# Hybrid attention and mLSTM encoder layer: more projection work ahead of the short sequence's gates and state products, and the long sequence's small loads moved from SyncE's queue to GpSimd's

## The chip, the cores and the metric

One core of a Trainium2 chip runs the whole layer. The metric is the device time of one execution in microseconds (us); lower is better.

## The reference, cut to what matters

Two sequences, 1024 ("short", s = 0) and 2048 tokens ("long", s = 1), each with 16 learned meta tokens ahead, go through the same layer in float32. One input projection feeds two branches, a neighbourhood attention (8 heads of 64) and a bidirectional mLSTM (4 heads of 128); both results are gated, projected, merged and projected once more.

```python
proj = xn @ w_in + b_in                      # 1024 -> 6672 columns
na_q, na_k, na_v, na_z, ml_qk, ml_v, ml_z, ml_o, ml_g, mg = split(proj)
ya = (neighbourhood_attention(na_q, na_k, na_v, rpb) * silu(na_z)) @ w_a
yb = (mlstm(ml_qk, ml_v, ml_g, ml_o, conv_w, head_g) * silu(ml_z)) @ w_b
ga, gb = split(sigmoid(mg))
y = (ga * ya + gb * yb) @ w_out
return h + rmsnorm(y, g_post)
# mlstm, chunk by chunk, both directions: the state is a decayed sum of weighted products
#   C_new = fs * C + isc * (w * v)^T k      with w, fs, isc from the gates ml_g
#   h = (S v + e * C q) / max(|den|, exp(-m))
```

## The kernel before, in words

TensorE's order is written by hand (`manual_schedule` for PE); the other engines' orders come from a scheduler that simulates the program. PE's order is woven in `run()` out of two generators. `dense` yields the big projections piece by piece: groups of input projections, the Strassen-like gate products (lines 787 to 790 and 988 to 990), and last the "final" blocks. Each final block takes 512 tokens: output gates times the two branches' projections (128x512 matmuls at lines 218 to 220, from `yh`, `yl`), then the product with `w_out` (128x256 matmuls at lines 1953 to 1955). A dense matmul triple computes one float32-like product out of high and low halves (`xh`, `xl`, `whl`). `sparse` yields the four mixer stages in the order of `STEPS`: mLSTM of the short sequence, attention of the short, mLSTM of the long, attention of the long. At every `yield` of `sparse`, dense pieces worth that cost (times `A_S`, 1.15 for the short and 0.91 for the long sequence) are put into PE's order before the sparse work goes on; they cover the time in which VectorE, ScalarE and the DMAs prepare the next sparse step. Costs are counted with 0.235 us for a 128x512 matmul and 0.12 for a 128x256.

An mLSTM stage has three parts, which this case names by their functions.

- `ml_gates`: the gate inputs are loaded as `g_t` (lines 1320, 1321), cumulative sums are taken by matmuls with a triangle (line 1347), and per-chunk values are transposed on PE (line 1400 for `g_uR`, line 1409 for e and w).
- `ml_states`, per head and per 256 tokens: a convolution input `raw` (line 1437) and values `va` (line 1507) are loaded, the keys are convolved (`kf`, line 1534), transposed on PE (line 1574), split into `kth` (ScalarE, line 1577) and `ktl` (VectorE, line 1578), and multiplied with the weighted values `vwh`, `vwl` (six matmuls `sm<-vwh,kth`, lines 218 to 220). `ktl` is the input of the third, sixth of these.
- `ml_outputs`, per head and per 256 tokens: loads of `raw`, `kf` (line 1620), two `um` (line 1626), and per 512 tokens `tog`, `szg` (lines 1638, 1639); `kh` (ScalarE, line 1665), scores `sc<-q,kh` (line 1703), the decay matrix on VectorE and ScalarE out of `um` (lines 1673 to 1723), products with `v2`.

In the attention, the last step of each head pair and 512 tokens is PE's line 1288, then `yg` by ScalarE (line 1295) and VectorE (1302, 1304), and a store to `ya` (line 1305). `yload` loads it again for the final block (`yl`, line 1850; `yh` by ScalarE, line 1871; the low half by VectorE, line 1855). Final block 3 of the long sequence is the last and needs `ya` of the last 512 tokens. In `final`, the products with `yb` (k = 4 to 7) stand ahead of those with `ya` (k = 0 to 3). If a needed `yl` hasn't been ordered yet, `final` yields True, and `run` goes on with sparse work alone until it has.

Nearly all loads and stores are issued by SyncE (SP) in program order, among them the dense side's weights (`whl`, lines 304 and 310) and activations (`xh`, `xl`, lines 944 and 953); GpSimd (POOL) issues some 200 others.

Of the kernel before, what the change touches and what calls it, by code (L numbers as in the profile page):

```python
# [18 lines left out]
P = 128  # L19
# [9 lines left out]
BIG = 1e30  # L29
# [9 lines left out]
BL = CB * P  # L39
# [96 lines left out]
A_N, A_D, A_A, A_G, A_S = (1.08, 0.93), 1.63, 1.79, 1.3, (1.15, 0.91)  # L136


class K:
# [1169 lines left out]
    def ml_gates(self, s, keep, mp, res):  # L1309
        nc = self.nc  # L1310
# [4 lines left out]
        kt = lambda n: keep.tile([P, NC_, 4], F32, name=n, bufs=1)  # L1315
        gt = t("g_t", [P, NC_, 16])
        for d in range(2):
            nc.gpsimd.memset(gt[:, 0, 8 * d:8 * d + 4], -BIG)
            nc.gpsimd.memset(gt[:, 0, 8 * d + 4:8 * d + 8], 1.0e4)
        nc.sync.dma_start(gt[:NM, 0, :], self.GA[s][0:NM, :])  # L1320
        nc.sync.dma_start(gt[:, 1:, :], self.GA[s][NM:, :].rearrange("(c p) g -> p c g", p=P))
        yield 11.0
        gv = gt.rearrange("p c (d k h) -> p d k c h", d=2, k=2)
        lf = t("g_lf", [P, 2, NC_, 4])
        e = t("g_e", [P, 2, NC_, 4])
# [18 lines left out]
        def one(d):  # L1344
            l2 = lf[:, d].rearrange("p c h -> p (c h)")
            pb = self.psum("sm", [P, 512])
            nc.tensor.matmul(pb[:, :NR], self.tri[:, d, :], l2, start=True, stop=True)
            bT = t(f"g_b{d}", [P, NC_, 4])
            nc.vector.tensor_copy(bT.rearrange("p c h -> p (c h)"), pb[:, :NR])
            aT = kt(f"g_a{d}")  # L1350
            nc.vector.tensor_tensor(aT, gv[:, d, 0], bT, op=ALU.subtract)
            aTf = aT.rearrange("p c h -> p (c h)")
            yield
            pa = self.psum("sm", [P, 512])
            nc.tensor.transpose(pa[:NR, :P], aTf, self.ident)
            aR = t("g_aR", [NR, P], bufs=2)
            nc.scalar.activation(aR, pa[:NR, :P], AF.Copy)
            yield
            cm = t("g_cm", [NR, P], bufs=2)
            rv = (lambda x: x) if d == 0 else (lambda x: x[:, ::-1])  # L1360
            nc.vector.tensor_tensor_scan(out=rv(cm), data0=rv(aR), data1=rv(aR), initial=-3.0e38, op0=ALU.max, op1=ALU.max)
            end = P - 1 if d == 0 else 0
            pg = self.psum("sm", [P, 512])
            nc.tensor.matmul(pg[0:1, :NR], self.ones[:, 0:1], l2, start=True, stop=True)
            rg = t("g_rg", [1, NR], bufs=2)
            nc.scalar.activation(rg, pg[0:1, :NR], AF.Copy)
            yield
            px = self.psum("sm", [P, 512])
            nc.tensor.transpose(px[0:1, :NR], cm[:, end:end + 1], self.ident[:NR, :NR])
            ra = t("g_ra", [1, NR], bufs=2)  # L1370
            nc.vector.tensor_tensor(ra, px[0:1, :NR], rg, op=ALU.add)
            me = t("g_me", [1, NR], bufs=2)
            mpv = t("g_mp", [1, NR], bufs=2)
            nc.gpsimd.memset(mpv, 0.0)
            yield
            for h in range(4):
                w = slice(h, NR, 4)
                nc.vector.tensor_tensor_scan(out=rv(me[:, w]), data0=rv(rg[:, w]), data1=rv(ra[:, w]), initial=0.0,
                                             op0=ALU.add, op1=ALU.max)
            if d == 0:  # L1380
                nc.vector.tensor_copy(mpv[:, 4:], me[:, :NR - 4])
            else:
                nc.vector.tensor_copy(mpv[:, :NR - 4], me[:, 4:])
            yield
            pm = self.psum("sm", [P, 512])
            nc.tensor.transpose(pm[:NR, 0:1], mpv, self.ident[0:1, 0:1])
            mpc = t("g_mpc", [NR, 1], bufs=2)
            nc.vector.tensor_copy(mpc, pm[:NR, 0:1])
            uR = t("g_uR", [NR, P], bufs=2)
            nc.vector.tensor_scalar(uR, cm, mpc, -1.0, op0=ALU.max, op1=ALU.mult)  # L1390
            nc.sync.dma_start(self.UD[s][d][:, :], uR)
            uend = t("g_ue", [NR, 1], bufs=2)
            nc.vector.tensor_copy(uend, uR[:, end:end + 1])
            nc.scalar.activation(cm, uR, AF.Exp, bias=mpc)
            nc.scalar.activation(aR, aR, AF.Exp, bias=uend)
            fs = t("g_fs", [NR, 1], bufs=2)
            nc.scalar.activation(fs, uend, AF.Exp, bias=mpc)
            yield
            pu = self.psum("sm", [P, 512])
            nc.tensor.transpose(pu[:, :NR], uR, self.ident[:NR, :NR])  # L1400
            em = kt(f"g_em{d}")
            nc.vector.tensor_tensor(em.rearrange("p c h -> p (c h)"), pu[:, :NR], bT.rearrange("p c h -> p (c h)"), op=ALU.subtract)
            nc.scalar.activation(em, em, AF.Exp)
            dg = t("g_dg", [NR, NR], bufs=2)
            nc.vector.tensor_scalar(dg, self.ident[:NR, :NR], fs, None, op0=ALU.mult)
            yield
            for name, x in (("e", cm), ("w", aR)):
                pe = self.psum("sm", [P, 512])
                nc.tensor.transpose(pe[:, :NR], x, self.ident[:NR, :NR])
                eT = kt(f"g_{name}T{d}")  # L1410
                nc.vector.tensor_copy(eT.rearrange("p c h -> p (c h)"), pe[:, :NR])
                out[d][name] = eT
                yield
            pf = self.psum("sm", [P, 512])
            nc.tensor.matmul(pf[:, :NR], self.ones[:NR, :], dg, start=True, stop=True)
            fsb = kt(f"g_fb{d}")
            nc.vector.tensor_copy(fsb.rearrange("p c h -> p (c h)"), pf[:, :NR])
            out[d].update(a=aT, em=em, f=fsb)
# [8 lines left out]
    def conv_load(self, src, c0, n, T):  # L1427

        nc = self.nc
        L = NM + T  # L1430
        raw = self.keep.tile([P, BL + 2], F32, name="raw", bufs=2)
        a, b = max(c0 - 1, 0), min(c0 + n + 1, L)
        if a > c0 - 1:
            nc.gpsimd.memset(raw[:, 0:1], 0.0)
        if b < c0 + n + 1:
            nc.gpsimd.memset(raw[:, n + 1:n + 2], 0.0)
        nc.sync.dma_start(raw[:, a - c0 + 1:b - c0 + 1], src[:, a:b])
        return raw

    def conv(self, raw, h, is_k, n):  # L1440
# [13 lines left out]
    def ml(self, s):  # L1454
        tc, nc = self.tc, self.nc
        T, self.seq = SEQLEN[s], s
        NB = T // BL
        with tc.tile_pool(name=f"mg{s}", bufs=1, side="right", reuse_waits="tile") as keep:
            with tc.tile_pool(name=f"mt{s}", bufs=1, side="right", reuse_waits="tile") as mp:
# [43 lines left out]
    def vload(self, s, h, tok, np_, nch):  # L1503
        nc = self.nc
        va = self.vas[0]
        self.vas = self.vas[1:] + [va]
        nc.sync.dma_start(va[:np_, :nch, 0:P],
                          self.MV[s][tok:tok + np_ * nch, h * P:(h + 1) * P].rearrange("(c p) f -> p c f", p=np_))
        return va

    def ml_states(self, s, h, g, NB, sts):

        nc, mp = self.nc, self.mlp
# [53 lines left out]
        for i in range(N):  # L1567
            n, c0 = seq[i]
            nch, np_ = max(1, n // P), min(n, P)
            conv_a(i + 1)  # L1570
            kf = kfs.pop(i)
# [9 lines left out]
            conv_b(i + 1)  # L1581
            vsplit(i + 1)
            yield A_D
            vwh, vwl = vws.pop(i)
            if not c0:
                pd = self.psum("sm", [P, 512])
# [4 lines left out]
            b = (c0 - NM) // BL  # L1591
# [5 lines left out]
            for j in range(CB - 1, -1, -1):  # L1597
# [6 lines left out]
                if cc > 0:  # L1604
                    nc.vector.scalar_tensor_tensor(sts[(cc - 1) // CB][:, (cc - 1) % CB, 130:260], sts[b][:, j, 130:260],
                                                   g[1]["f"][:, 1 + cc, h:h + 1], pd[:, 130:260], op0=ALU.mult, op1=ALU.add)
            yield A_D

    def ml_outputs(self, mp, s, h, g, NB, sts, norms):

# [4 lines left out]
        def load(b):  # L1615
            if b < NB:
                t0 = b * BL
                raws[b] = self.conv_load(self.MQ[s][h], NM + t0, BL, SEQLEN[s])
                kfs[b] = kf = self.keep.tile([P, BL], F32, name="kf", bufs=2)
                nc.sync.dma_start(kf, self.KF[s][h][:, t0:t0 + BL])  # L1620
                ums[b] = []
                for d in range(2):
                    um = mp.tile([P, CB, P], F32, name="um", bufs=4)
                    ud = self.UD[s][d]
                    src = bass.AP(tensor=ud.tensor, offset=ud.offset + ((1 + b * CB) * 4 + h) * P, ap=[[0, P], [4 * P, CB], [1, P]])
                    nc.sync.dma_start(um, src)
                    ums[b].append(um)

        def vnext(b):
# [3 lines left out]
        def gates(b):  # L1633

            if b % 2:
                tzs[b // 2] = [mp.tile([P, 4, P], F32, name=n, tag="tz", bufs=2) for n in ("tog", "szg")]
                x, z = tzs[b // 2]
                nc.sync.dma_start(x, self.TO[s][(b - 1) * BL:(b + 1) * BL, h * P:(h + 1) * P].rearrange("(c p) f -> p c f", p=P))
                nc.sync.dma_start(z.rearrange("p a b -> p (a b)"), self.SZ[s][h][:, (b - 1) * BL:(b + 1) * BL])

        def conv_a(b):
            if b < NB:
# [564 lines left out]
```

## Time and profile before

| what | value |
|---|---|
| time, median of 3 runs | 2666.21 us (2662.89 to 2666.56) |
| the profiled execution's own time | 2665.67 us |
| its span | 2663.9 us, 46683 instructions |
| granted TensorE clock, mean | 0.997 |
| PE busy | 2635.1 us (99%) |
| VectorE (DVE), ScalarE (ACT), GpSimd (POOL) busy | 72%, 53%, 7% of the span |
| DMA | 800.47 MB, 300 GB/s; SP's queue q1 697.24 MB, POOL's queue q0 100.25 MB |

PE is busy nearly all the time, so the time is PE's work plus the gaps in it. A row of the list of waits says: the engine and line that waited, what it waited for, the microseconds in total, how often, and the longest. In the timeline a row is start, duration, engine, line, operation, tile out<-in, and in brackets the idle time before it and what ended it. In the table of stretches a row gives each engine's busy time and, as PEclk, the clock granted to TensorE as a share of full speed, then the share of the DMA engines and GB/s.

### The profile page before, as it was taken

The page shows a single profiled execution, that of the slowest core. Times are in us where ns is not written, and L with a number is a line of the kernel's source. Part 1 is how long each engine was busy: PE and PEld are TensorE (multiplying, and loading weights), DVE is VectorE, ACT ScalarE, POOL GpSimd, SP SyncE. Part 2 cuts the span into 40 slices and gives each one's busy share as a digit, 9 for nine tenths or more (in the row PEclk, how much of TensorE's full clock was granted, in tenths as well). Part 3 has the DMA queues.
Part 4 walks back from the last instruction along what each step waited for, and adds up shares of the span by engine and source line. Part 5 has one row for each costly group of instructions (what it writes and reads, how often), then busy time and mean ns, then how long its engine had stood idle before and what let it go on. Part 6 is the DMA issues. An engine that isn't in the chain of part 4 may idle for free.

```text
span 2663.9 us, 46683 instructions
## 1 busy us (share of the span) xinstructions
PE 2635.1 (99%) x15928; PEld 2328.5 (87%) x15928; DVE 1915.0 (72%) x5070; ACT 1423.7 (53%) x3292; POOL 196.3 (7%) x418
## 2 busy tenths in 40 slices
PE   9999999999999999999999999999999999999998
PEld 7898897899988999878888888878889898989888
DVE  5655678788776877546676776857478889797854
ACT  5423555555445554546665676656366655656521
POOL 0111131011301124000000000000000000000000
PEclk9999999999999999999999999999999999999999
DMA  9899988799866999978889998899899899898965
GB/s 371 328 332 337 332 302 303 279 339 344 313 218 242 352 324 309 317 230 268 261 269 342 370 295 260 282 348 324 275 323 321 283 306 286 284 306 266 326 244 206
DMA packets 393517, 800.47 MB, mean 300 GB/s; under 512 B 50528, under 2 KB 173360, under 8 KB 389440
## 3 DMA queue, kind: packets, MB, share of 16 engines
q1 hardware_dynamic: 361728, 697.24, 77.9%
q0 software_dynamic: 31552, 100.25, 10.2%
q8 instruction: 126, 2.06, 0.3%
q14 instruction: 111, 0.91, 0.1%
HBM read 543.72 MB, written 253.60 MB: 299 GB/s over the span
## 4 chain that ended last, share of the span: by engine, by line
PE 91%; DMA 4%; DVE 3%; ACT 1%; issue 1%; SPq 0%; DVEq 0%; ACTq 0%
PE pj L218 10%; PE pj L220 10%; PE pj L219 10%; PE pj L988 8%; PE pj L990 8%; PE pj L989 8%; PE pj L787 5%; PE pj L789 5%; PE pj L788 5%; PE pj L1954 3%; PE pj L1953 3%; PE pj L1955 3%; PE sm L1288 3%; PE tr L1273 2%; PE sm L220 1%; PE sm L219 1%
## 5 line engine op out<-in xcount | busy, mean ns | idle before, releaser
L218 PE MATMUL pj<-xh,whl 128*128 128x512 f32 (+1 forms) x960 | 369.7, 385 | 3.1 <-ACT xh L445 2.5
L220 PE MATMUL pj<-xh,whl 128*128 128x512 f32 (+1 forms) x960 | 361.0, 376 | 0.0
L219 PE MATMUL pj<-xl,whl 128*128 128x512 f32 (+1 forms) x960 | 360.3, 375 | 0.2 <-DVE xl L446 0.2
L787 PE MATMUL pj<-whl,xh 128*128 128x256 f32 (+1 forms) x1152 | 329.0, 286 | 0.0
L789 PE MATMUL pj<-whl,xl 128*128 128x256 f32 (+1 forms) x1152 | 325.3, 282 | 0.0
L788 PE MATMUL pj<-whl,xh 128*128 128x256 f32 (+1 forms) x1152 | 324.9, 282 | 0.0
L1953 PE MATMUL pj<-whl,mh 128*128 128x256 f32 x768 | 218.3, 284 | 1.1 <-DMA whl<-w 1.1
L787 PEld LDWEIGHTS pj<-whl,xh 128*128 128x128 f32 x1152 | 217.1, 188 | 0.4
L788 PEld LDWEIGHTS pj<-whl,xh 128*128 128x128 f32 x1152 | 217.0, 188 | 0.2
L789 PEld LDWEIGHTS pj<-whl,xl 128*128 128x128 f32 x1152 | 217.0, 188 | 0.0
L1954 PE MATMUL pj<-whl,mh 128*128 128x256 f32 x768 | 216.3, 282 | 0.0
L1955 PE MATMUL pj<-whl,mlo 128*128 128x256 f32 x768 | 215.5, 281 | 0.0
L218 PEld LDWEIGHTS pj<-xh,whl 128*128 128x128 f32 x960 | 181.2, 189 | 35.3 <-ACT xh L445 3.4
L220 PEld LDWEIGHTS pj<-xh,whl 128*128 128x128 f32 x960 | 181.2, 189 | 35.0
L219 PEld LDWEIGHTS pj<-xl,whl 128*128 128x128 f32 x960 | 181.8, 189 | 30.4 <-issue 1.0
L988 PE MATMUL pj<-xh,whl 128*128 128x512 f32 x512 | 206.7, 404 | 1.3 <-ACT pj L1005 1.1
L990 PE MATMUL pj<-xh,whl 128*128 128x512 f32 x512 | 202.0, 395 | 0.0
L989 PE MATMUL pj<-xl,whl 128*128 128x512 f32 x512 | 201.1, 393 | 0.0
L1280 DVE TENSOR_TENSOR pts<-tr,pts 96x384 fp32r<-96x384 f32 (+2 forms) x192 | 118.6, 618 | 63.8 <-ACT pts L1275 62.4
L1275 ACT ACTIVATE pts<-tr 96x384 fp32r<-96x384 f32 (+2 forms) x192 | 103.5, 539 | 101.7 <-PE tr L1273 101.1
L218 PE MATMUL pj<-yh,whl 128*128 128x512 f32 x384 | 154.1, 401 | 0.0
L219 PE MATMUL pj<-yl,whl 128*128 128x512 f32 x384 | 151.5, 395 | 0.7 <-DVE yl L1855 0.7
(380 smaller groups left out, 6824.9 us busy)
## 6 DMA issues: line engine op xcount, KB each, us to landing
whl<-w SPq DMA_DIRECT2D x131, 1024.0 KB
whl<-q SPq DMA_DIRECT2D x112, 512.0 KB
w<-whl SPq DMA_DIRECT2D x36, 1024.0 KB
wraw<-wu SPq DMA_DIRECT2D x48, 512.0 KB
gt<-st SPq DMA_DIRECT2D x96, 256.0 KB
tg<-gt SPq DMA_DIRECT2D x96, 256.0 KB
q<-po POOLq DMA_DIRECT2D x26, 512.0 KB, 7.3
xt<-xt SPq DMA_DIRECT2D x24, 512.0 KB
```

The lines of the kernel that those rows point to most:

```text
L218: mm(out, ah, bh, start=start, stop=False)
L219: mm(out, ah, bl, start=False, stop=False)
L220: mm(out, al, bh, start=False, stop=stop)
L787: nc.tensor.matmul(o, xh, wh, start=k == 0, stop=False)
L788: nc.tensor.matmul(o, xh, wl, start=False, stop=False)
L789: nc.tensor.matmul(o, xl, wh, start=False, stop=k == KT - 1)
L988: mm(bank, w[:, 0, k], xh[:, k], start=fresh and k == 0, stop=False, skip_group_check=True)
L989: mm(bank, w[:, 0, k], xl[:, k], start=False, stop=False, skip_group_check=True)
L990: mm(bank, w[:, 1, k], xh[:, k], start=False, stop=k == 3, skip_group_check=True)
L1953: nc.tensor.matmul(o, mh[:, k, xs], wh, start=clear > 0 and k == 0, stop=False)
L1954: nc.tensor.matmul(o, mh[:, k, xs], wl, start=False, stop=False)
L1955: nc.tensor.matmul(o, ml[:, k, xs], wh, start=False, stop=clear < 2 and k == KT - 1)
```

## The change

1. `ml_gates`, both sequences: the fills of `g_t` and `mpv` are made by VectorE and not by GpSimd. The first yield is 14.0 for the long sequence (11.0 before, and for the short still). For the short sequence one more `yield` stands ahead of the transposes at line 1400 and one ahead of those at line 1409.
2. `self.mq` is GpSimd's queue for the long sequence and SP's for the short. `raw`, `va`, `kf` of the outputs, `um`, `tog` and `szg` are loaded through it. So 261 DMA rows of the long mLSTM leave SP's order and 251 rows more stand in POOL's.
3. `ml_states`, short sequence: the yield behind the state products stands ahead of them now, so that three pieces and not two lie between a transposition and its products, and the next transposition follows the products at once. The meta item at the end of each head gets one yield more.

```diff
-            nc.gpsimd.memset(gt[:, 0, 8 * d:8 * d + 4], -BIG)
-            nc.gpsimd.memset(gt[:, 0, 8 * d + 4:8 * d + 8], 1.0e4)
+            nc.vector.memset(gt[:, 0, 8 * d:8 * d + 4], -BIG)
+            nc.vector.memset(gt[:, 0, 8 * d + 4:8 * d + 8], 1.0e4)
...
-        yield 11.0
+        yield 14.0 if s else 11.0
...
-            nc.gpsimd.memset(mpv, 0.0)
+            nc.vector.memset(mpv, 0.0)
...
             yield
+            if s == 0:
+                yield
             pu = self.psum("sm", [P, 512])
             nc.tensor.transpose(pu[:, :NR], uR, self.ident[:NR, :NR])
...
             yield
+            if s == 0:
+                yield
             for name, x in (("e", cm), ("w", aR)):
...
-        nc.sync.dma_start(raw[:, a - c0 + 1:b - c0 + 1], src[:, a:b])
+        self.mq.dma_start(raw[:, a - c0 + 1:b - c0 + 1], src[:, a:b])
...
+        self.mq = nc.gpsimd if s else nc.sync
...
-        nc.sync.dma_start(va[:np_, :nch, 0:P],
+        self.mq.dma_start(va[:np_, :nch, 0:P],
...
             vsplit(i + 1)
             yield A_D
+            if s == 0:
+                yield A_D
             vwh, vwl = vws.pop(i)
...
-            yield A_D
+            if s:
+                yield A_D
...
-                nc.sync.dma_start(kf, self.KF[s][h][:, t0:t0 + BL])
+                self.mq.dma_start(kf, self.KF[s][h][:, t0:t0 + BL])
...
-                    nc.sync.dma_start(um, src)
+                    self.mq.dma_start(um, src)
...
-                nc.sync.dma_start(x, self.TO[s][(b - 1) * BL:(b + 1) * BL, h * P:(h + 1) * P].rearrange("(c p) f -> p c f", p=P))
-                nc.sync.dma_start(z.rearrange("p a b -> p (a b)"), self.SZ[s][h][:, (b - 1) * BL:(b + 1) * BL])
+                self.mq.dma_start(x, self.TO[s][(b - 1) * BL:(b + 1) * BL, h * P:(h + 1) * P].rearrange("(c p) f -> p c f", p=P))
+                self.mq.dma_start(z.rearrange("p a b -> p (a b)"), self.SZ[s][h][:, (b - 1) * BL:(b + 1) * BL])
```

PE has the same instructions in both kernels. What moves is where the sparse ones stand among the dense ones: every extra yield puts dense matmuls ahead, and the sparse work stays later by them to the end.

First place, PE in the state products of the short sequence's first head. Before, the six products (`sm<-vwh,kth` and so on) are followed by dense matmuls:

```order
2012 L218 MATMUL sm<-vwh,kth 128x260
2013 L219 MATMUL sm<-vwl,kth 128x260
2014 L220 MATMUL sm<-vwh,ktl 128x260
2015 L218 MATMUL sm<-vwh,kth 128x260
2016 L219 MATMUL sm<-vwl,kth 128x260
2017 L220 MATMUL sm<-vwh,ktl 128x260
2018 L218 MATMUL pj<-xh,whl 128x512
```

In the changed kernel the next transposition of keys (line 1574 before, 1579 here) follows them at once:

```order
2005 L218 MATMUL sm<-vwh,kth 128x260
2006 L219 MATMUL sm<-vwl,kth 128x260
2007 L220 MATMUL sm<-vwh,ktl 128x260
2008 L218 MATMUL sm<-vwh,kth 128x260
2009 L219 MATMUL sm<-vwl,kth 128x260
2010 L220 MATMUL sm<-vwh,ktl 128x260
2011 L1579 MATMUL tr<-ident,kf 128x128 x2
```

The six dense matmuls that stood between the products and the next transposition stand behind that transposition now: 24 lie between it and its products, where 18 did.

Second place, SP's queue at the start of the long mLSTM. Before, `raw` and `va` of the first two items stand between the constants (`tri`, `trim`) and the gate inputs:

```order
746 L1461 DMA tri_14199<-tri 128x256
747 L1463 DMA trim_14201<-trimask 128x256
748 L1437 DMA raw_14209<-mk10_208 128x257
749 L1507 DMA va0_14203<-mv1_247 128x2x128
750 L1437 DMA raw_14213<-mk10_208 128x258
751 L1507 DMA va1_14204<-mv1_247 128x2x128
752 L1320 DMA g_t_14216<-gg1_259 16x16
753 L1321 DMA g_t_14216<-gg1_259 128x16x16
```

In the changed kernel:

```order
751 L1466 DMA tri_14253<-tri 128x256
752 L1468 DMA trim_14255<-trimask 128x256
753 L1320 DMA g_t_14270<-gg1_259 16x16
754 L1321 DMA g_t_14270<-gg1_259 128x16x16
755 L304 DMA whl_14292<-q4s1_12172 128x1024
```

The four loads are gone from SP's order, and `g_t` follows the constants.

Third place, PE at the end of the long attention. Line 1288 with three matmuls is the last attention product of the kernel. Before, it stands within the last `w_out` products of final block 2; 84 matmuls of 128x256 and then 12 products of block 3 with `yb` follow before the first with `ya`:

```order
14159 L1954 MATMUL pj_30796<-whl_30537,mh_29589 128x256
14160 L1955 MATMUL pj_30796<-whl_30537,mlo_29590 128x256
14161 L1288 MATMUL sm_30759<-pts_30738,vt_30380 128x256 x3
14162 L1953 MATMUL pj_30796<-whl_30537,mh_29589 128x256
14163 L1954 MATMUL pj_30796<-whl_30537,mh_29589 128x256
```

In the changed kernel it stands behind those 12 products of block 3 with `yb` (`pj_30929`), directly ahead of the 12 with `ya` (`pj_30970`, k = 0 to 3, three matmuls each):

```order
14255 L219 MATMUL pj_30929<-yl_30195,whl_30638 128x512
14256 L220 MATMUL pj_30929<-yh_30194,whl_30638 128x512
14257 L1288 MATMUL sm_30887<-pts_30884,vt_30508 128x256 x3
14258 L218 MATMUL pj_30970<-yh_30194,whl_30638 128x512
14259 L219 MATMUL pj_30970<-yl_30195,whl_30638 128x512
```

Between the last attention product and the first matmul on its result (k = 3) lay 84 matmuls of 128x256 and 21 of 128x512; now it is 9 of 128x512.

## Prediction

> **What bounds the kernel now.** I read the page first, then the list of waits, then the timeline around each wait, and last the table of stretches for the clock. The page's first part:
>
> ```profile
> PE 2635.1 (99%) x15928; PEld 2328.5 (87%) x15928; DVE 1915.0 (72%) x5070; ACT 1423.7 (53%) x3292; POOL 196.3 (7%) x418
> ```
>
> PE does the same matmuls in both kernels, so the change can only move the 28.8 us of the span in which PE isn't busy, and the time in which its clock is low. PE's waits, those that the change can reach:
>
> ```profile
> PE sm L220 <- DVE ktl L1578: 4.8, 3, 2.6
> PE sc L1703 <- ACT kh L1665: 2.8, 1, 2.8
> ...
> PE sm L1347 <- issue: 1.9, 1, 1.9
> PE pj L1953 <- DMA whl<-w: 1.1, 1, 1.1
> ...
> PE sm L1409 <- DVE g_eT L1411: 1.0, 1, 1.0
> PE pj L219 <- DVE yl L1855: 0.7, 1, 0.7
> PE sm L1400 <- DVE g_uR L1390: 0.5, 1, 0.5
> PE pj L218 <- DMA whl<-w: 0.5, 1, 0.5
> PE sm L1409 <- DVE g_em L1402: 0.3, 1, 0.3
> ...
> PE sc L1704 <- DVE kl L1666: 0.2, 1, 0.2
> ```
>
> The reader is to see that the three parts of the change each have their waits here: the short sequence's gates (lines 1400 and 1409, 1.8 us), its state products (`ktl`, 4.8 us), the long sequence's gates (line 1347, 1.9) and its outputs (`kh` and `kl`, 3.0). Three of these cost more than the wait, as the stretches behind them show:
>
> ```profile
> core 0: us, PE busy (x) PEld busy (x) DVE busy (x) ACT busy (x) POOL busy (x), PEclk, DMA share, GB/s
> ...
> 430.00:435.00 5.00, 4.10 (x21) 3.43 (x22) 5.00 (x12) 3.60 (x9) 0.53 (x1) 1.00 0.01 3
> 435.00:440.00 5.00, 2.67 (x13) 2.03 (x11) 5.00 (x9) 4.70 (x9) 0.00 (x1) 1.00 0.83 261
> 440.00:445.00 5.00, 4.70 (x19) 3.95 (x20) 5.00 (x10) 4.04 (x10) 0.00 (x0) 0.66 0.92 320
> ...
> 1195.00:1200.00 5.00, 5.00 (x19) 3.53 (x18) 2.44 (x8) 2.03 (x7) 0.00 (x0) 0.66 0.98 312
> ...
> 1797.00:1802.00 5.00, 2.04 (x6) 1.66 (x7) 1.20 (x4) 2.92 (x8) 0.00 (x0) 0.73 0.87 283
> 1802.00:1807.00 5.00, 5.00 (x18) 4.25 (x18) 3.44 (x10) 2.44 (x8) 0.00 (x0) 0.59 0.92 330
> ```
>
> After each the granted clock is 0.59 to 0.73. Work lost so is busy time times one less the clock: 4.70 x 0.34 = 1.6 us at 440, 5.00 x 0.34 = 1.7 at 1195, 2.04 x 0.27 + 5.00 x 0.41 = 2.6 at 1797. The Trainium skill's page "TensorE: Matmul & The Clock Gate", section "What's actually happening", lets the clock fall only after an idle window of some 3.4 us; these stretches disagree, with 0.66 after a wait of 1.9 us, and the measurement decides. By the page those 5.9 us would stay and the sum below would be about 5 us worse.
>
> **The change, part by part.** All terms are against the profiled execution's own 2665.67 us (its span 2663.9 and 1.8 around it), which is 0.5 under the median of the runs.
>
> *Short gates.* Each extra yield puts six dense 128x512 matmuls, 1.4 us, ahead of the waiting transposes. Each of the waits (1.0, 0.5, 0.3) is shorter. VectorE, which makes `g_uR` and `g_em`, gets only the fills in addition. A fill isn't shown on VectorE; at the 0.36 us of a small operation there (line 1330, below) five would be 1.8 us, ahead of the gates' chain and beside dense work: nothing, at most what the cover doesn't take. **Minus 1.8** (1.0 to 1.8).
>
> *Short states.* The waits of 430 and 440 us:
>
> ```profile
> 430.90 0.39 PE L220 MATMUL sm<-vwh,ktl 128*128 128x260 f32 x1 [1.23 <-DVE ktl L1578]
> ...
> 440.30 0.39 PE L220 MATMUL sm<-vwh,ktl 128*128 128x260 f32 x1 [2.63 <-DVE ktl L1578]
> ```
>
> VectorE is busy through all of 430 to 445 in the stretches above, with preparations for the next projection group that stand ahead of `ktl`. Six more matmuls between transposition and product move the need of `ktl` 1.4 us later against its source. That covers 1.23 and half of 2.63, but the total of dense work per round is unchanged, so VectorE's surplus is not carried off, only its place. With the wait goes the clock's 1.6. Ends: 0 (VectorE is late as before) and 3.9 + 1.6 = 5.5. I take **minus 3.5**, nearer to the upper end, since the stretch of 430 keeps clock 1.00 beside its wait of 1.23 us, so that a wait cut to that size costs no clock. The third of the three waits, 4.8 - 3.9 = 0.9 us, is shorter than the new cover: **minus 0.9** (0 to 0.9).
>
> *Long gates.* Line 1347 waits at 1193.68 for a chain that starts with `g_t`:
>
> ```profile
> 1182.02 0.43 SPq L1437 DMA_DIRECT2D raw<-mk  x1
> ...
> 1184.01 0.41 SPq L1320 DMA_DIRECT2D g_t<-gg  x1
> 1184.46 0.42 SPq L1321 DMA_DIRECT2D g_t<-gg  x1
> ```
>
> ```profile
> 1188.62 0.36 DVE L1330 TENSOR_SCALAR g_lf<-g_t 128x68 f32<-128x68 f32 x2 [1.08 <-DMA g_t<-gg]
> ```
>
> `raw` and `va` go to POOL's queue, so `g_t` is issued 2.0 us earlier, and 3.0 more of cost at the first yield puts 2.7 us of dense work ahead. Together 4.7 us against a wait of 1.92: gone, and the clock's 1.7 with it. `raw` then lands some 2 us later than on SP (below), which delays a convolution that no matmul waits for here. **Minus 3.6** (1.9 to 3.6).
>
> *Long outputs.* The wait of 2.81 us at 1797 comes from a load on SP's queue:
>
> ```profile
> 1784.79 2.84 SPq L953 DMA_DIRECT2D xl<-xl  x1
> 1787.73 2.35 SPq L1620 DMA_DIRECT2D kf<-kf  x1
> ```
>
> ```profile
> 1799.33 0.42 ACT L1665 ACTIVATE kh<-kf 128x256 fp32r<-128x256 f32 x1 [1.62 <-DMA kf<-kf]
> ```
>
> `kf` (128x256 float32, 128 KB) took 11.6 us behind the large loads of a new projection group (`xl` and its kind), where `raw`, of the same size, took 3.9 (1182.02 above to its use):
>
> ```profile
> 1185.90 0.51 ACT L1446 ACTIVATE cv<-raw,cw 128x256 f32<-128x256 f32 x1 [1.75 <-DMA raw<-mk]
> ```
>
> POOL did nothing in these stretches (0.00, x0). Landings of its queue on the page:
>
> ```profile
> q<-po POOLq DMA_DIRECT2D x26, 512.0 KB, 7.3
> ...
> nv<-stT POOLq DMA_DIRECT2D x96, 64.0 KB, 5.7
> ```
>
> At 5.7 to 7.3 `kf` is there by 1795, before PE needs it at 1797. The wait of 3.0 and the clock's 2.6 go, 5.6 at most, nothing if `um` or another load is late instead. I take **minus 4.5**.
>
> *The same queue everywhere else.* Against that, every small load of the long mLSTM now takes POOL's latency, some 2 us over the 3.9 of a quiet SP queue. An issue costs POOL little:
>
> ```profile
> L846 POOL DMA_DIRECT2D nv<-stT x96 | 55.3, 579 | 83.4 <-DVE stT L805 31.5 <-DVE stT L803 21.0 <-DVE sm L1265 4.4
> ```
>
> 251 more of 0.58 us are 146 us of POOL's time, and POOL is 7% busy. The Trainium skill speaks against the move: its page "SBUF — State Buffer", section "Who interferes with whom", says that descriptor making for GpSimd's DMAs is locked out while VectorE runs a copy, cast or tensor_scalar in a two-port mode. In 430 to 435 VectorE is busy for all 5 us and POOL's one issue took 0.53, under its mean; that stretch's long operations take two tensors, so it is no full test, and by the page each issue could start later by one such operation, inside the range that follows. What these latencies reach is `um`:
>
> ```profile
> 1610.95 1.43 SPq L1626 DMA_DIRECT2D um<-ud  x2
> ```
>
> ```profile
> 1616.14 0.43 DVE L1673 TENSOR_TENSOR um<-um,trim 128x256 f32<-128x256 f32 x1 [1.85 <-DMA um<-ud]
> L1673 DVE TENSOR_TENSOR um<-um,trim 128x256 f32<-128x256 f32 x96 | 38.9, 418 | 12.8 <-DMA um<-ud 12.8
> ```
>
> `um` is issued when its buffer is free and was 1.85 us late there already, without any wait of PE. VectorE has waited 12.8 us in all for it. Two us more per block of 256 tokens will make VectorE wait more often; PE has 12 to 24 matmuls of cover at each step. I put **plus 2** (from -1.6, if SP's relief ends the two waits for `whl`, to +16, in the rivals).
>
> *The end of the long attention.* The sparse work runs later against the dense by 54 to 60 matmuls at the end, and so the last result of the attention meets the final block that reads it. The chain, before:
>
> ```profile
> 2554.15 0.52 PE L1288 MATMUL sm<-pts,vt 104*128 104x256 f32 x3
> ...
> 2557.15 0.33 SPq L1305 DMA_DIRECT2D ya<-yg  x1
> ...
> 2559.51 0.59 SPq L1850 DMA_DIRECT2D yl<-ya  x1
> ```
>
> ```profile
> 2566.00 0.62 ACT L1871 ACTIVATE yh<-yl 128x512 fp32r<-128x512 f32 x1
> ...
> 2569.64 0.69 DVE L1855 TENSOR_TENSOR yl<-yl,yh 128x512 fp32r<-128x512 f32 x1
> 2570.38 0.50 PE L219 MATMUL pj<-yl,whl 128*128 128x512 f32 x1 [0.73 <-DVE yl L1855]
> ```
>
> From the end of the last product, 2554.67, it is 2.5 us to the store's issue, 2.4 to the load's (the store must have landed), then the load, at least 2 and at most 6.5 us (2566.00), estimated at 4 from `raw` and `g_t` (3.9 and 4.2), then 0.6 and 0.7: 10.2 us. By the order of the instructions 9 matmuls of 128x512 stand in between, 0.235 us each by the kernel's own count, so 2.1 us; before, 84 of 128x256 and 21 of 128x512 covered the whole chain. The first matmul needs `yh` only, 0.2. **PE waits 10.2 - 2.1 - 0.2 = 7.9 us**, 0.7 of which is there today, and the clock falls as after 1797, some 2.0: **plus 9.2** (7 to 12.5).
>
> Sum: -1.8 - 3.5 - 0.9 - 3.6 - 4.5 + 2 + 9.2 = -3.1, so **2662.6 us**. The gains are real and most of them are given back at the end.
>
> **Rivals.**
> *The end is not exposed.* The load could be in time if the scheduler has the last `ya` stored sooner, or some other cover comes. Against it: the dependence is direct and the position is fixed by hand. Without the 9.2 the time is 2653.4.
> *POOL's latency decides in the long outputs (slower).* In 4 heads x 8 blocks, `um` and `kf` arrive one step late, VectorE's decay matrix is late, and PE waits at the products with `v2`. It decides once the landing exceeds the lead by more than the cover, about 5.2 us (1610.95 to 1616.14) plus some 2 us. POOL's 5.7 to 7.3 stand just at that. At 0.5 us of wait per block that is 16 in place of my 2: 2676.6. For it: 1.85 us of lateness exist already. Against it: the 12.8 us that VectorE has waited for `um` cost PE nothing outside the stretch at 1797.
> *The two large waits move and don't go.* VectorE's burst still holds `ktl`, and the new group's large loads still hold whatever is loaded beside them, on any queue (DMA share 0.87 to 0.92 there). Without the 3.5 and 4.5 the time is 2670.6.
>
> **How the numbers follow.** Forecast 0.46: 2656 to 2669 by its own terms; rival one 0.14; rival two 0.25; rival three 0.15. A difference of 0.2%, 5.3 us, is about what a measurement of this kernel can tell from no change. Faster by more (under 2660.9): half of the forecast, 0.22, and rival one, 0.14: 0.36. Slower (over 2671.5): rival two, 0.25, a third of rival three, 0.05, and 0.01 of the forecast: 0.31. Within: 0.33. The range, 2653 to 2677, takes in rivals one and two at their prices.
>
> **What would show it.** In the profile after: no wait at lines 1400, 1409 and 1347 (their numbers shifted by the edit), clock 1.00 behind the long gates; `ktl` under 1.5 us in all; no wait of `kh` over 1 us. A wait of 6 to 10 us of PE for `yh` or `yl` in the last final block, at the same product as the 0.7 of today, and a stretch under 0.7 of the clock behind it: if it's missing, rival one. VectorE's waits for `um` at several times 12.8 us, and waits of PE at the products with `v2` in the long outputs: rival two. I am wrong most easily in the +2, which rests on POOL latencies of other transfers, and in the length of the load at the end.

## The result and the profile after

The changed kernel took 2684.03 us (median of 4 runs, 2683.23 to 2686.97) against 2665.7 us (4 runs, 2662.89 to 2666.56): ratio 1.0071, 95% interval [1.0059, 1.0084], 18.3 us slower. I had forecast 2662.6 with a range up to 2677. The profiled execution's span is 2682.5 us, 18.6 more than before.

The first line of the page of the changed kernel:

```profile
PE 2641.8 (98%) x15928; PEld 2332.2 (87%) x15928; DVE 1913.5 (71%) x5082; ACT 1419.0 (53%) x3292; POOL 366.1 (14%) x670
```

PE is idle for 40.7 us (28.8 before) and busy 6.7 us longer with the same matmuls. Some 3 us of these are a lowered clock (its mean is 0.996 for 0.997); the rest isn't taken apart. PE's waits in the changed kernel (who waited, for what, total, times, longest):

```profile
PE sm L1288 <- ACT prb L1256: 8.2, 8, 4.0
PE pj L218 <- ACT yh L1879: 5.6, 1, 5.6
PE sm L219 <- DVE vwl L1556: 2.9, 2, 1.9
PE sm L1288 <- DVE yg L1302: 2.9, 2, 2.7
PE sc L1711 <- ACT kh L1673: 1.8, 1, 1.8
...
PE sm L218 <- DVE cv L1453: 1.4, 1, 1.4
...
PE sm L1288 <- DVE pts L1280: 1.0, 2, 0.7
PE sm L220 <- DVE ktl L1583: 0.9, 2, 0.6
PE sm L1413 <- ACT g_cm L1394: 0.7, 1, 0.7
...
PE sm L1355 <- DVE g_a L1351: 0.5, 1, 0.5
```

The waits that the change was read to remove did shrink: `ktl` from 4.8 to 0.9, `kh` from 2.8 to 1.8 (now at 345 us, another place), line 1347 and the short gates' lines are gone. In their place stand 5.6 for `yh`, a wait that was forecast, and 12.1 at line 1288, the last product of each attention unit (2.2 before).

To place the loss, I took for every PE row the time to the next row, less the median of that time for the same kind of row in the kernel before, and added up the excess by stage (a stage runs from its first PE row to the next stage's). It counts waits and lowered clock alike. In us:

| kernel (median time) | opening | short mLSTM | short attention | long mLSTM | long attention | after its last product |
|---|---|---|---|---|---|---|
| before (2665.7) | 3.3 | 17.1 | 5.2 | 25.4 | 13.4 | 1.5 |
| changed (2684.0) | 3.1 | 16.6 | 6.8 | 23.0 | 28.0 | 9.3 |

The sums differ by 21 us where the spans differ by 18.6, since a moved row changes what is usual behind it; the table is good to some 2 us. Each row of it, and each such excess below, is one profiled execution, whose own time can lie some us from the kernel's median. All of the loss lies in the long attention (+14.6) and behind its last product (+7.8), two stages in which the change edits nothing. What reaches them is the shift: the sparse work stands 54 to 60 dense matmuls later. The scheduler's orders of the other engines differ there too.

The place that the prediction priced, at the end of the long attention, in the changed kernel's timeline:

```profile
2577.76 0.52 PE L1288 MATMUL sm<-pts,vt 104*128 104x256 f32 x3
...
2580.66 0.33 SPq L1305 DMA_DIRECT2D ya<-yg  x1
...
2582.68 0.33 SPq L1858 DMA_DIRECT2D yl<-ya  x1
2585.28 0.63 ACT L1879 ACTIVATE yh<-yl 128x512 fp32r<-128x512 f32 x1 [6.58 <-DMA yl<-ya]
...
2585.97 0.80 PE L218 MATMUL pj<-yh,whl 128*128 128x512 f32 x1 [5.59 <-ACT yh L1879]
```

And the stretches behind it (PE busy, then the other engines; PEclk is the third number from the end):

```profile
2585.00:2590.00 5.00, 4.03 (x9) 2.92 (x10) 2.07 (x3) 1.23 (x2) 0.00 (x0) 0.50 0.14 20
2590.00:2595.00 5.00, 5.00 (x21) 4.03 (x20) 1.38 (x2) 0.03 (x1) 0.00 (x0) 0.89 0.77 295
```

2.4 us to the store, 2.0 to the load, 2.6 for the load, 0.7 for `yh`: the chain of the prediction, with a load of 2.6 in place of 4. Then 4.03 x 0.5 + 5.00 x 0.11 = 2.6 us by the clock.

### The profile page after: what moved, and what is told of

Its sections match the earlier page's. It is cut to its first block, busy times and chain, and to the rows that moved or that the text cites. A ratio compares the mean times of both kernels' runs of the same rounds, so it can differ in the third digit from the quotient of the medians.

```text
span 2682.5 us, 46762 instructions
## 1 busy us (share of the span) xinstructions
PE 2641.8 (98%) x15928; PEld 2332.2 (87%) x15928; DVE 1913.5 (71%) x5082; ACT 1419.0 (53%) x3292; POOL 366.1 (14%) x670
## 4 chain that ended last, share of the span: by engine, by line
PE 88%; DMA 5%; DVE 3%; ACT 2%; issue 1%; SPq 0%; DVEq 0%; ACTq 0%; POOLq 0%
PE pj L218 10%; PE pj L220 10%; PE pj L219 10%; PE pj L988 7%; PE pj L990 7%; PE pj L989 7%; PE pj L787 5%; PE pj L789 5%; PE pj L788 5%; PE sm L1288 3%; PE pj L1962 3%; PE pj L1961 3%; PE pj L1963 3%; PE tr L1273 2%; DMA kf<-kf 1%
## 5 line engine op out<-in xcount | busy, mean ns | idle before, releaser
L218 PE MATMUL pj<-yh,whl 128*128 128x512 f32 x384 | 155.9, 406 | 5.6 <-ACT yh L1879 5.6
L220 PE MATMUL pj<-yh,whl 128*128 128x512 f32 x384 | 153.2, 399 | 0.0
```

The source lines that it names most:

```text
L218: mm(out, ah, bh, start=start, stop=False)
L220: mm(out, al, bh, start=False, stop=stop)
```

## The experiments

Two theories. **Place:** what costs is the later place of the long attention and its end against the dense work, whatever moved it. **Queue:** what costs is GpSimd's queue, through which the long mLSTM's loads now come late (the prediction's slower rival).

**The shift alone.** The kernel before, with one push of dense work at the start of the long attention (in `run`):

```diff
             if isinstance(w, tuple):
+                acc += 12.7 if w == ("n", 1, 0) else 0.0
```

> The kernel before, with one thing added: at the start of the long attention 12.7 us of dense work (54 matmuls of 128x512) is put ahead once, so that the long attention stands against the dense work as it does in the changed kernel, and nothing else of the change is there. Theory 1, the later place of the sparse work against the dense is what costs: 2680 to 2688 us, with the waits of the changed kernel in the long attention (some 4 us at line 1288 near 1969) and 5 to 6 us for yh at the last final block. Theory 2, the long mLSTM's loads on GpSimd's queue cost: 2664 to 2668, no such waits.

Measured: 2685.48 us against 2665.87, ratio 1.0071 [1.0056, 1.0086]. One line that changes no stage but the long attention's place gives the whole loss; counted as in the table, some 10 us of it lie in the long attention and 8 behind its last product. Its waits:

```profile
PE pj L218 <- ACT yh L1871: 6.0, 1, 6.0
PE sm L1288 <- ACT prb L1256: 5.7, 6, 3.3
```

**The change without the queue.** The changed kernel with `self.mq = nc.sync`.

> The changed kernel with all small loads of the long mLSTM back on SP's queue. Theory 1 (place): 2681 to 2688 us, as the changed kernel. Theory 2 (queue): 2662 to 2668.

Measured: 2699.97 us, ratio 1.0126 [1.011, 1.0141]: 16 us slower than the changed kernel, outside what either theory expected. The queue doesn't cost; in the changed kernel it saves. Without it PE waits longest for a load of the long outputs:

```profile
PE sc L1711 <- ACT kh L1673: 9.7, 3, 6.1
```

**The queue alone.** The kernel before, with `self.mq` as in the change, and no other edit.

> The kernel before with only the small loads of the long mLSTM moved to GpSimd's queue; no yield is added or moved. Theory 1 (place): 2660 to 2668 us, the wait of 2.8 us for kh in the long outputs smaller or gone. Theory 2 (queue): 2680 to 2686.

Measured: 2665.52 us, ratio 0.9999 [0.9989, 1.0008]. `kh` is gone from its waits, but the long gates wait 6.25 us where they waited 1.92. In this kernel GpSimd still fills `g_t`, now behind four DMA issues. The last fill on its queue, SP's rows from the load of line 1321 to that of line 1320, and PE:

```profile
1177.08 0.14 POOL L1319 MEMSET g_t<- 128x4 f32 x1
```

```profile
1183.65 0.43 SPq L1321 DMA_DIRECT2D g_t<-gg  x1
1184.13 3.94 SPq L304 DMA_DIRECT2D whl<-q  x1
1188.17 0.85 SPq L723 DMA_DIRECT2D nk<-st  x2
1189.11 0.44 SPq L1320 DMA_DIRECT2D g_t<-gg  x1
```

```profile
1199.64 1.10 PE L1347 MATMUL sm<-g_lf,tri 128*128 128x68 f32 x4 [6.25 <-issue]
```

The fills were done at 1177.2, six us before any load of `g_t` was issued. The load of line 1320, which writes into filled rows, nevertheless stands behind that of line 1321 and behind two other rows in SP's order, one of which takes 3.94 us; in the kernel before it stood ahead of line 1321's. The order is the scheduler's.

**The whole change, shift given back.** Dense work per yield of the long mLSTM scaled, so that the long attention stands within 12 matmuls of its place before:

```diff
-            acc += w * A_S[self.seq] if self.seq is not None else w
+            acc += w * A_S[self.seq] * (0.979 if self.seq and self.kind == "ml" else 1.0) if self.seq is not None else w
```

> The whole change, but the dense work per yield of the long mLSTM is scaled by 0.979, so that the 54 matmuls are given back by its end and the long attention and the last final block stand as in the kernel before. Theory 1 (place): 2661 to 2668 us, the wait for yh back to under 1 us. Theory 2 (queue): 2681 to 2686.

Measured: 2668.65 us (2661.88 to 2674.07, 10 runs), ratio 1.0011 [1.0001, 1.0021]. Without the shift some 3 of the 18 us are left of the loss, and nothing of a gain. The excess was 18.7 in the long mLSTM (25.4 before), 1.4 at the end, but 22.4 in the long attention: 9 of the changed kernel's 14.6 us are still there, although no product of it stands more than 12 matmuls from its old place. The theory of the place alone doesn't give these 9.

**The end alone.** The push of 12.7 us late, at three of 32 head units ahead of the end (in the unit loop of `na`; `run` adds `self.give` once):

```diff
+                self.give = 12.7 if s and u == 116 else 0.0
```

> The kernel before, with 12.7 us of dense work put ahead once, but only three of 32 head units ahead of the end of the long attention. The last product stands as late as in the changed kernel, the rest of the long attention as before. If the exposed last result is its own loss of some 8 us: 2672 to 2676 us, with a wait of 5 to 6 us for yh and a clock near 0.5 behind it. If the whole 19.6 us of the shift come from the end: 2684. If the end costs nothing: 2666.

Measured: 2673.4 us against 2666.84, ratio 1.0028 [1.0018, 1.0039]: +6.6 us. The wait and the clock behind it:

```profile
PE pj L218 <- ACT yh L1872: 5.2, 1, 5.2
```

```profile
2575.00:2580.00 5.00, 2.77 (x6) 1.94 (x7) 1.44 (x3) 0.63 (x1) 0.00 (x0) 0.50 0.19 52
```

**The end given back.** The changed kernel, with dense work held back over the last quarter:

```diff
+                self.give = -0.4 if s and 96 <= u < 128 else 0.0
```

> The changed kernel, with 12.8 us of dense work held back in small parts over the last quarter of the long attention, so that the last product stands as in the kernel before. If the end is its own loss of 8 us: 2674 to 2678 us, no wait for yh over 1 us, and the waits of the long attention's first three quarters stay. If the long attention's waits and the end are one loss: 2666. If holding back only makes the gaps earlier: 2684.

Measured: 2678.5 us, ratio 1.0046 [1.0031, 1.0061], 5.5 less than the changed kernel. No wait for `yh` is left (excess at the end 1.4), and the long attention keeps 27.9. The end is a loss of its own, some 6 to 7 us by these two runs.

**A small shift.** 5.64 us in place of 12.7, at the start of the long attention (`self.give = 5.64 if s and u == 0`).

> The kernel before, with 5.6 us (24 matmuls of 128x512) and not 12.7 put ahead at the start of the long attention. The last result keeps over 8 us of cover, so the end costs nothing. If any other place of the long attention against the dense work loses about as much as the changed kernel's (11 us beside the end): 2674 to 2680. If the loss grows with the shift: 2669 to 2672. If the changed kernel's place is merely unlucky: 2664 to 2668.

Measured: 2675.43 us, ratio 1.0032 [1.002, 1.0045]: +8.6. The excess is 22.7 in the long attention (13.4 before) and 4.6 at the end. There I was wrong that the end costs nothing: `yh` is waited for 1.9 us. These 9.3 us in the long attention are of the slowest of six executions, 2680.18, which is 4.8 over the median. By the medians 8.6 us, less some 3 at the end, leave 5 to 6 for 24 matmuls, where 54 cost 10 to 15. So whether the loss grows in step with the shift isn't settled.

**The queue with the fills.** The queue alone, and the fills of `g_t` and `mpv` by VectorE.

> The kernel before with the small loads of the long mLSTM on GpSimd's queue and the gates' fills on VectorE; no yield is added. With the loads alone the wait at the long gates had grown to 6.2 us, since the load of g_t waits for a fill that GpSimd makes behind its DMA issues. If that is its cause: that wait under 2 us and 2658 to 2663 us. If the growth is the queue's latency: 2665 and a wait of 6 still.

Measured: 2658.09 us (2655.79 to 2660.44), ratio 0.9969 [0.9959, 0.998], some 8 us faster than before. Line 1347's wait, and loads of one size by queue in this one kernel (KB each, median us from issue to landing). SP's rows are the short sequence's loads, another stage:

```profile
PE sm L1347 <- issue: 1.1, 1, 1.1
```

```profile
va<-mv POOLq DMA_DIRECT2D x64, 128.0 KB, 5.9
um<-ud POOLq DMA_DIRECT2D x64, 128.0 KB, 6.0
...
va<-mv SPq DMA_DIRECT2D x32, 128.0 KB, 8.1
um<-ud SPq DMA_DIRECT2D x32, 128.0 KB, 7.7
```

Here SP issues line 1320's load at 1182.03, ahead of line 1321's. So the wait went with the fills, as expected; but not for the reason that my expectation names, since with GpSimd's fills the load was late by its place in SP's order and not by a fill that it waited for. The excess in the long mLSTM is 17.7, 7.7 less than before. VectorE's waits for `um`, 12.8 us before, are 8.7. This is the part of the change that gains.

**The short parts alone.** The extra yields and moved products of the short sequence, and the shift given back in the short attention (its costs times 0.966).

> The kernel before with the short sequence's extra yields and moved state products only, and the dense work per yield of the short attention scaled by 0.966, so that the shift is given back before the long mLSTM. If the short parts are worth little by themselves and the place of the later stages is all that cost: 2661 to 2667 us, the waits for ktl cut from 4.9 to about 1. If the short parts cost by themselves: over 2669.

Measured: 2667.21 us (2660.97 to 2673.68), ratio 1.0007 [0.9995, 1.0018]. `ktl` falls to 0.8, and others take its place at once:

```profile
PE sc L1710 <- ACT kh L1672: 4.4, 2, 2.6
...
PE sm L218 <- DVE cv L1453: 1.4, 1, 1.4
...
PE sm L220 <- DVE ktl L1582: 0.8, 2, 0.6
```

**The long parts alone.** The changed kernel without the short sequence's yields: queue, fills, and 14.0 at the long gates, which shifts what follows by 12 matmuls.

> The changed kernel without the short sequence's yields: the queue, the fills and 14.0 at the long gates, so a shift of only 12 matmuls (2.8 us) from the long gates to the end. The queue and the fills alone gave 2658.1. If even a small shift of the long attention costs about as much as a large one: 2664 to 2670. If it takes more than that: 2656 to 2660.

Measured: 2667.97 us (2662.05 to 2672.11), ratio 1.0006 [0.9996, 1.0016]. Queue and fills without the 14.0 gave 0.9969: 3.0 more at one yield costs their whole gain, 9.9 us by the medians. Its profiled execution, one of the fastest at 2662.71, shows 19.1 in the long attention, 3.9 more than with queue and fills; the 5 us more of a usual execution aren't placed.

**The shift behind a burst.** In the shift alone, PE's longest wait at line 1288 ended at 1972.15. ScalarE's rows ahead of it:

```profile
1966.06 0.83 ACT L1214 ACTIVATE kd<-kx 64x768 fp32r<-64x768 f32 x1
1966.80 1.14 ACT L1871 ACTIVATE yh<-yl 128x512 fp32r<-128x512 f32 x2
...
1968.52 0.84 ACT L1216 ACTIVATE kd<-kd 64x768 fp32r<-64x768 f32 x1
...
1969.67 0.62 ACT L1221 ACTIVATE vt<-vr 96x512 fp32r<-96x512 f32 x1
1970.19 0.71 ACT L707 ACTIVATE st<-st,bfh 128x512 f32<-128x512 f32 x1
1970.93 0.69 ACT L707 ACTIVATE st<-pj,bfh 128x512 f32<-128x512 f32 x1
1971.52 0.49 ACT L1256 ACTIVATE prb<-sm,mx 128x288 f32<-128x288 f32 x1
```

`yh` (line 1871) belongs to the dense side: eight splits for the first final block, here at 1961 to 1968. `kd` and `vt` (1214, 1216, 1221) prepare the next head unit of the attention. The `prb` of 1971.52, which the list names as what PE waited for, stands in one queue behind both. VectorE's half of `vt`, an input of this product, was done only at 1971.97, behind splits of the same burst:

```profile
1969.70 1.28 DVE L1855 TENSOR_TENSOR yl<-yl,yh 128x512 fp32r<-128x512 f32 x2
...
1971.30 0.67 DVE L1226 TENSOR_TENSOR vt<-vr,vt 96x512 fp32r<-96x512 f32 x1
```

In the kernel before, the same preparation ran at 1950 to 1953, ahead of the eight splits:

```profile
1950.99 0.85 ACT L1216 ACTIVATE kd<-kd 64x768 fp32r<-64x768 f32 x1
```

```profile
1959.04 1.18 ACT L1871 ACTIVATE yh<-yl 128x512 fp32r<-128x512 f32 x2
```

So the experiment pushes the 12.7 us only behind that place (`self.give = 12.7 if s and u == 40`).

> The kernel before with 12.7 us of dense work put ahead in the long attention, as in the run with the shift alone, but behind its tenth head unit, after the eight splits of yh and yl for the first final block (1959 to 1968 us). If the collision of that burst with a head unit's preparation made the wait of 3.3 us at line 1288 and the lowered clock behind it: 2677 to 2681, no wait near 1970. If that wait has another cause: 2684 to 2687.

Measured: 2677.46 us, ratio 1.0042 [1.0027, 1.0057], 8 us less than with the push ahead of the burst. PE is busy throughout there, at full clock (first fence), where the shift alone (second) waits 3.3 us and loses 2.85 x 0.36 = 1.0 us by the clock, and 5.00 x 0.33 = 1.7 in the 5 us behind (0.67):

```profile
1965.00:1970.00 5.00, 5.00 (x28) 4.16 (x27) 5.00 (x13) 4.90 (x11) 0.00 (x0) 1.00 1.02 372
1970.00:1975.00 5.00, 5.00 (x27) 4.19 (x26) 4.90 (x12) 3.57 (x7) 0.00 (x0) 1.00 1.03 412
```

```profile
1965.00:1970.00 5.00, 3.82 (x21) 2.98 (x20) 5.00 (x12) 4.95 (x11) 0.00 (x0) 1.00 1.02 397
1970.00:1975.00 5.00, 2.85 (x8) 2.46 (x9) 3.58 (x10) 2.55 (x6) 0.00 (x0) 0.64 1.02 388
```

So 6 of the 8 us are this place. That the push ahead of it makes the wait is shown; that the splits in the two queues do it is read from the rows, and no run moved the splits alone.

**All parts, no shift.** The short parts with their shift given back in the short attention, the queue and the fills, and 11.0 at the long gates.

> The short parts with their shift given back in the short attention, plus the queue and the fills for the long mLSTM, without 14.0 at its gates. If the parts add up once the place of the later stages is kept: 2653 to 2659 us. If the order of the other engines shifts anyway and costs: 2660 to 2668.

Measured: 2659.97 us (2658.82 to 2662.09), ratio 0.9979 [0.997, 0.9988], a little above my range for "the parts add up". The short parts add nothing to queue and fills.

## Why the prediction was wrong

*The failed step* is the one headed "The end of the long attention". It saw that the sparse work runs 54 to 60 matmuls later and priced that at its last product alone, as if every other place of the long attention were as good as the one before. The runs show otherwise: the shift alone costs 19.6 us, of which the end is some 7 (the late push gave 6.6) and the long attention most of the rest. The sum had no term for it.

*Term by term*, forecast against the table: the short parts -6.2, and the short mLSTM's excess fell by 0.5; the long gates, outputs and the queue together -6.1, and the long mLSTM's fell by 2.4; the end +9.2, and it rose by 7.8; the rest of the long attention 0, and it rose by 14.6.

*The end itself* was right in kind and near in size: plus 9.2 forecast, 7.8 by the table, a wait of 5.6 for 7.9, mostly since the load took 2.6 us for 4; the clock took 2.6 for 2.0. Rival one, no exposure, is ruled out.

*The term of plus 2 for the queue* and rival two, which carried my chance of slower: no cost of the queue shows. I took 3.9 us from one quiet load as SP's landing; in the run with queue and fills the short sequence's loads of 128 KB take 7.7 and 8.1 by SP, the long's 5.9 and 6.0 by GpSimd's queue. The stages differ, so this doesn't compare the queues cleanly (SP's `raw` lands in 3.5 us for the queries and 10.6 for the keys); the run's time does. VectorE's waits for `um` rose with the whole change from 12.8 to 20.5 us, as rival two had it, without PE's stage losing; with queue and fills alone they fell to 8.7. That the time came out slower, as rival two said, is no support for it: the shift alone, on SP's queue, is as slow.

```profile
L1681 DVE TENSOR_TENSOR um<-um,trim 128x256 f32<-128x256 f32 x96 | 39.0, 417 | 20.6 <-DMA um<-ud 20.5
```

*Long outputs, minus 4.5,* was right about the load behind the large ones: queue and fills took 7.7 us off the long mLSTM and 8 off the kernel, which is the outputs and the gates together. (The clock's part at 1797 was 3.1 us, not 2.6: PE was busy for 6.1 of the 6.83 us that the clock was at 0.50, from 1799.27.) In the changed kernel the stage gains 2.4 only, because at its new place it meets the large loads elsewhere (a wait of 1.9 for `vwl` at 1774, with clock 0.66 in the 5 us from there).

*Long gates, minus 3.6:* the wait at line 1347 went, 0.5 and 0.7 us at two later lines came, and the 3.0 of extra cost at the yield, which I counted as cover alone, is by the run without the short parts a shift that costs more than it covers. The fills, which I priced only as work on VectorE, are needed for the queue to gain: with GpSimd's the load of `g_t` gets a later place in SP's order, and the wait is 6.25.

*Short parts, minus 6.2 together:* the waits went as forecast, the time didn't. With the shift given back their effect is 1.0007 [0.9995, 1.0018]. A wait of 1.4 us for `cv` came at the products themselves, with clock 0.75 in the stretch from 445 to 450 us, so the clock's 1.6 was not gained; and 1.8 (changed kernel) to 4.4 (short parts alone) for `kh`. I had said that VectorE's surplus is only moved, and counted on the upper end all the same. So rival three, that the two large waits move and don't go, came true in part; it doesn't give the time, since its price only takes gains away.

What stays open: the place at 1970 is shown, some 6 of the 10 to 15 us. The wait of 1.8 at 2186 in the changed kernel stands at the same product in the shift alone (2.2 at 2190) and not with the shift given back, so it comes with the shift too. The one of 2.7 at 2306 isn't in the shift alone, and with the shift given back one of 2.6 stands at 2304, at the next head unit: the shift by itself doesn't make it. In the changed kernel and all runs, 14 of the 17 waits over 1.5 us at this line in the long attention stand at the first product of a head unit, the one that needs the unit's new `vt`; what delays it each time wasn't taken apart. Nor is it settled why the run with the shift given back loses 22.4 there, with PE's order within 12 matmuls of before; the other engines' orders come from the scheduler and differ, and no run held them fixed.

## What to carry to other kernels

When two streams are woven into one queue by hand, extra work put ahead in an early stage moves every later stage against the other stream; before pricing such an edit, look at what the other stream asks of the shared engines at each later place, and give the shift back where it isn't wanted. A wait that disappears from the list is no gain until the next input of the same instruction has been looked at. Small loads that stand behind large ones in one queue gain from a queue of their own, but what a scheduler then makes of every other queue's order has to be looked at too (here one load's place cost what the queue gained).

## What the runs showed of the hardware that was not expected

A wait of 5.6 us of PE was followed by a stretch at clock 0.50, one of 3.3 us by two at 0.64 and 0.67, and ones of 1.9 to 2.8 us by 0.59 to 0.73 (before). But behind 2.91 us, at 1969.58 in the run with the end given back, it stayed 1.00. The numbers between 0.50 and 1.00 are means over 5 us: in every trace here the clock is either, and the low stretches in mid-run last 3.41 us or a multiple. Within a run their starts lie whole multiples of 3.413 us apart: in the kernel before 440.76, then 221 of them to 1195.11 and 177 more to 1799.27. Cut along this grid, the window ahead of the fall at 1195.11 and the two windows that share the wait of 2.91 us are

```profile
1191.70:1195.11 3.41, 1.49 (x9) 1.31 (x9) 3.22 (x11) 2.29 (x4) 0.00 (x0) 1.00 1.02 355
1195.11:1198.52 3.41, 3.41 (x10) 2.57 (x9) 1.31 (x5) 1.29 (x4) 0.00 (x0) 0.50 0.99 298
```

```profile
1964.70:1968.11 3.41, 1.97 (x11) 1.35 (x9) 2.84 (x8) 3.34 (x8) 0.00 (x0) 1.00 1.04 413
1968.11:1971.53 3.42, 1.95 (x11) 1.73 (x12) 2.02 (x7) 1.88 (x6) 0.00 (x0) 1.00 1.06 379
1971.53:1974.94 3.41, 3.41 (x20) 2.87 (x19) 1.71 (x4) 1.10 (x4) 0.00 (x0) 1.00 1.01 311
```

PE is busy for 1.49 of 3.41 us (44%) in the first, and the next window runs at 0.50; it is busy for 57% in each of the other two, and no fall follows. Over the 13 traces that have such a fall between their first 40 us and last 15 us, all 38 windows at full clock with PE busy for up to 46% were followed by 0.50, four of the six between 47% and 49%, and one (56%) of all those above. So here a wait of 2 to 3 us cost the clock's 1.7 us more when it fell into one window, and nothing more when it was split over two.

Loads of 128 KB issued by GpSimd landed in 5.5 to 6.0 us (medians, in the run with queue and fills); SP's loads of about that size lay between 3.5 and 10.6 in the short sequence's stages.
